# Rotary tables built with positions along the row, and a norm factor spread through DRAM, in a two-layer decoder trunk on one Trainium2 core

## The chip, the cores and the metric

The kernel runs on one core of one Trainium2 chip. The metric is the device time of one execution in microseconds, median of several runs; before the change it is 650.1 us (three runs, 649.99 to 650.54). The engines of the core are named as in the profile: PE (TensorE matmuls; PEld is its weight load), DVE (VectorE), ACT (ScalarE), POOL (GpSimd) and SP (SyncE, which only issues DMAs here).

## The reference

A trunk of two layers over 256 positions of width 1024, batch 1. Each layer is an attention mixer, a cross attention over 256 memory rows and a gated MLP with a short convolution, each behind an RMS norm and a residual. What the change touches:

```python
def rope(x, positions):
    half = HEAD_DIM // 2
    inv_freq = ROPE_THETA ** (-jnp.arange(half, dtype=jnp.float32) / half)
    ang = positions.astype(jnp.float32)[:, None, :, None] * inv_freq
    cos, sin = jnp.cos(ang), jnp.sin(ang)
    xf = x.astype(jnp.float32)
    x1, x2 = xf[..., :half], xf[..., half:]
    return jnp.concatenate([x1 * cos - x2 * sin, x2 * cos + x1 * sin], axis=-1).astype(x.dtype)
...
# layer 0: heads 0-7 stick-breaking (no rotary), heads 8-15 block-sparse with rotary q and k
o_moba = moba_attention(rope(q[:, N_SB_HEADS:], positions),
                        rope(k[:, N_SB_HEADS:], positions), v[:, N_SB_HEADS:])
...
# every layer: cross attention reads rmsnorm(mem)
h = h + memory_cross_attention(rmsnorm(h, norm_xa_g[layer]), rmsnorm(mem, norm_mem_g[layer]), ...)
```

A head is 64 wide, so there are 32 frequencies. The RMS norm's gains are folded into what is multiplied, and its factor, one number for each row (position or memory row), is applied to results.

## The kernel before

**Layout.** Activations lie turned: 128 features on the partitions, the 256 positions along the row (`P` = 128, `T` = 256). Two heads of 64 share a tile of 128 partitions. Every fp32 product is made of three matmuls (line 303): weights and activations are split into a rounded part (`whi`, `xh`) and a rest (`wlo`, `xl`). Weights come in blocks of 128x1024 by SP into `raw` (seven buffers); ACT writes `whi` in two halves (line 134), DVE `wlo` (line 135), five buffers each. So each block of weights costs PE 24 matmuls, ACT two copies and DVE two subtractions.

**Order.** PE's order is the program's order, written by hand: `VISITS` and a `Pipe` that counts half-steps of the projection loop say after which projection a pair of heads is multiplied, weighed and summed. DVE, ACT, POOL and SP are ordered by the framework's scheduler from the same program; each engine then runs its own queue strictly in that order.

**Layer 0's mixer** (up to about 110 us) projects q and k of eight pairs of heads and v of four groups. Pairs 0 to 3 are stick-breaking (`Stick`): PE multiplies q and k and adds a mask (lines 378 to 383), ACT and DVE make `s` (lines 388 to 391) and split it into `sp` (ACT line 393, DVE line 394), PE multiplies `sp` by a triangle (lines 399, 401), ACT takes the exponential `pt` (line 403), PE multiplies `pt` by v (line 450). Pairs 4 to 7 are softmax heads whose q and k are rotated first.

**Rotary tables.** `rope_angles` (line 465) puts the positions on the partitions, 128 by 2, and makes a 128x64 tile of angles (two times 32 frequencies). The angle is reduced to a turn around zero in many small steps on DVE: rounding by a large constant (lines 478, 479), splitting the count of turns in two (481, 482) and subtracting pieces of two pi (486); a clamp ends it (489). It is a generator; a step of it runs at each half-step of the pipe. `rope_sines` (line 495) loads ACT's table for the sine, takes four sines, of the angle and of half the angle for each half of the positions, each with the 32 frequencies repeated four times so that a tile of 128x128 results, and loads the table of exponentials and logarithms again. `rope_tables` (line 506) turns the four tiles by PE's transposes into 128 features by 256 positions, copies them out of PSUM on ACT (with a sign by feature for the sine; the half angle's sine is squared), and DVE makes cos = 1 - 2 sin^2(half) and both tables times the row's norm factor (`scaled`). For pair 4 the tables are used after the swap of halves (`rope`, POOL and DVE), for pairs 5 to 7 in the evacuation itself (`evac_turned`).

**The memory's factor.** `mem.rows` loads the memory's rows and squares them (half on ACT, half on DVE); `mem.sums` makes the factor as a column, 128x2 (`rcol`: DVE line 280, a power on POOL line 284). `mem.spread` (line 288) makes it a row on all partitions (`rrow`): two PE transposes of a broadcast column (line 291) into the `po` bank and an ACT copy (line 294). Its readers are the evacuations of the memory's keys, `mk` (line 354).

Of the kernel before, what the change touches and what calls it, by code (L numbers as in the profile page):

```python
# [9 lines left out]
F32 = mybir.dt.float32  # L10
F32R = mybir.dt.float32r
BF16 = mybir.dt.bfloat16
I32 = mybir.dt.int32
AF = mybir.ActivationFunctionType
ALU = mybir.AluOpType
AX = mybir.AxisListType

P = 128
T = 256
D = 1024  # L20
KD = D // P
DH = 64
# [21 lines left out]
C_CONV = 64  # L44
C_BF = C_CONV + 2 * 4 * 2 * KF
C_FREQ = C_BF + 1
C_SIGN = C_FREQ + DH // 2
N_SMALL = C_SIGN + 1


# [29 lines left out]
def trunk(ctx: ExitStack, tc: tile.TileContext, a: dict, out: bass.AP):  # L80
    nc = tc.nc
# [9 lines left out]
    act = pool("act", 1)  # L91
    parts = pool("parts", 1)
    qkv = pool("qkv", 1)
    xin = pool("xin", 1)
    shift(64)
    wsp = pool("wsp", 5)
    tmp = pool("tmp", 2)
# [5 lines left out]
    NX, NG, NP, NB = 8, 16, 12, 8  # L103

    def bank(pl, tag, width=512):
        return pl.tile([P, 512], F32, tag=tag, name=tag)[:, :width]
# [7 lines left out]
    def order(later, earlier):  # L114
        tc.add_manual_dep(later.ins, earlier.ins.name,
                          mybir.DependencyInfo(mybir.DependencyClass.NoSync, mybir.DependencyReason.DATA),
                          reason="order")
# [121 lines left out]
    class Stats:  # L239
# [45 lines left out]

        def spread(self, ps=None):
            ps = ps or self.ps
            for t in range(2):  # L290
                nc.tensor.transpose(ps[:, t * P:(t + 1) * P], self.col[:, t:t + 1].broadcast_to([P, P]), ident)
            bufs = 1 if self.keep else 2
            self.row = act.tile([P, T], F32, tag="rrow" + self.keep, name="rrow", bufs=bufs)
            nc.scalar.copy(self.row, ps[:, :T])
# [168 lines left out]
    cos = cst.tile([P, T], F32, name="cos")  # L463

    def rope_angles():
        f = lambda n, dt=F32: xin.tile([P, T], dt, tag="gh", name=n, bufs=NG)[:, :DH]
        pi, ang, kk, kh = f("ri", I32)[:, :2], f("ra"), f("rk"), f("rh")
        pf = kk[:, :2]
        nc.sync.dma_start(pi, a["positions"])
        eng = nc.vector  # L470
        yield
        eng.tensor_copy(pf, pi)
        for t in range(2):
            eng.tensor_scalar(ang[:, t * DH // 2:(t + 1) * DH // 2], small[:, C_FREQ:C_SIGN], pf[:, t:t + 1], None,
                              op0=ALU.mult)
        for parts in (True, False):
            yield
            eng.tensor_scalar(kk, ang, 1.0 / TWO_PI, MAGIC, op0=ALU.mult, op1=ALU.add)
            eng.tensor_scalar(kk, kk, -MAGIC, None, op0=ALU.add)
            if parts:  # L480
                eng.tensor_scalar(kh, kk, MAGIC * 2048.0, -MAGIC * 2048.0, op0=ALU.add, op1=ALU.add)
                eng.tensor_tensor(kk, kk, kh, op=ALU.subtract)
            for c in _pieces():
                yield
                for n in (kh, kk) if parts else (kk,):
                    eng.scalar_tensor_tensor(ang, n, -c, ang, op0=ALU.mult, op1=ALU.add)
        yield
        pi_f = float(np.nextafter(np.float32(np.pi), np.float32(0)))
        eng.tensor_scalar(ang, ang, pi_f, -pi_f, op0=ALU.min, op1=ALU.max)
        angles.append(ang)  # L490

    angles = []


    def rope_sines(prev):
        s = tmp.tile([P, 2, 2, 4, DH // 2], F32, tag="wide", name="rs", bufs=5)
        for i, scale in enumerate((1.0, 0.5)):
            for t in range(2):
                x = angles[0][:, t * DH // 2:(t + 1) * DH // 2]
                prev, last = nc.scalar.activation(s[:, i, t], x.unsqueeze(1).broadcast_to([P, 4, DH // 2]), AF.Sin,  # L500
                                                  scale=scale), prev
                order(prev, last)
        order(nc.scalar.preload_act_table_set("natural_log_exp_and_others"), prev)
        angles.append(s)

    def rope_tables(st):
        ps = bank(psA, "acc")
        for i in range(4):
            nc.tensor.transpose(ps[:, i * P:(i + 1) * P], angles[1][:, i // 2, i % 2].rearrange("p a f -> p (a f)"),
                                ident)  # L510
        nc.scalar.activation(sin, ps[:, :T], AF.Copy, scale=small[:, C_SIGN:C_SIGN + 1])
        nc.scalar.activation(cos, ps[:, T:], AF.Square)
        nc.vector.tensor_scalar(cos, cos, -2.0, 1.0, op0=ALU.mult, op1=ALU.add)
        both = tmp.tile([P, 2 * T], F32, tag="wide", name="scaled", bufs=5)
        for i, x in enumerate((cos, sin)):
            scaled.append(both[:, i * T:(i + 1) * T])
            nc.vector.tensor_mul(scaled[i], x, st.row)
# [91 lines left out]
    def mixer(layer, st, xs):  # L609
# [20 lines left out]
        def visit(out, prod, weigh):  # L630
            if out:
                res = heads_out([(heads[n], pairs[n][2], (n % 2) * P) for n in out])
                for n, pr in zip(out, res):
                    outs[n] = pr
            for n in prod:
                q, k, _ = pairs[n]
                heads[n] = [Stick(i, q, k) if layer == 0 and n < 4 else
                            Soft(i, q, k, decays[2 * n + i] if decays else None) for i in range(2)]
            both_products([hd for n in prod for hd in heads[n]])
            for n in weigh:  # L640
                for i, hd in enumerate(heads[n]):
                    hd.weigh(nc.vector.tensor_copy if n > 5 and i else nc.scalar.copy)
            if layer == 0 and pipe.now == 8:
                rope_tables(st)
            if layer == 0 and pipe.now == 17:
                mem.spread(bank(psO, "po"))
            for n in prod:
                for hd in heads[n]:
                    hd.scores()

        if layer == 0:
            pipe.at(13, mem.sums)
            pipe.at(6, lambda: rope_sines(heads[1][1].last))
        for step, *work in VISITS[layer]:
            pipe.at(step, lambda work=work: visit(*work))

        for g in range(4):
# [27 lines left out]
            if g == 0 and layer == 0:  # L685

                accs = [accS() for _ in range(4)]
                for n, (xh, xl) in enumerate(xs):
                    b, o = b0[n // 2], (n % 2) * 4 * P
                    steps = [(b.hi, xh), (b.hi, xl), (b.lo, xh)]  # L690
                    for group in ((0, 1), (2, 3)) if n < 2 else (range(4),):
                        for m, (wt, x) in enumerate(steps):
                            for i in group:
                                product(accs[i], wt[:, o + i * P:o + (i + 1) * P], x, n == 1 and m == 2 and i == 3,
                                        start=n == 0 and m == 0, stop=n == KD - 1 and m == 2)
                b = [block(w[i]) for i in (2, 3, 6)]
                nc.sync.dma_start(const[:, :T], a["const"][:, :T])
                st.rows(a["xt"])
                b.append(block(w[7]))
                st.sums()  # L700
                pv = [proj_nat(b, xs, t, accA()) for t in range(2)]
                early = proj(b[2], 0, xs, accA(), hooks={9: lambda: st.spread(bank(psO, "po"))})
                late_constants()
                v = [evac_col(ps, st, t, "v", 6) for t, ps in enumerate(pv)]
                for i in range(2):
                    q, k = (evac_row(accs[2 * i + j], st, "qk"[j], j == 0) for j in range(2))
                    launch(i, q, k, v)
                steps = rope_angles()
                next(steps)
                for i in range(12):  # L710
                    pipe.at(1 + i // 3, lambda: next(steps, None))
                continue
            elif g == 0:
                f = bank(psO, "po", T)

                def rates():
                    gates(f)
                    st.sums()

                q, more = pair(0, ({20: rates}, {15: st.spread}))  # L720
                k = more()
                q, k = evac_row(q, st, "q", True), evac_row(k, st, "k", False)
                decay = decay_rows(f, st)
            else:
                q, k = pair(0)
# [358 lines left out]
def _layout(inp):  # L1084
# [19 lines left out]
    d["x"] = c(kt(inp["x"][0].T).reshape(P, -1))  # L1104
    d["mem"] = c(kt(inp["mem"][0].T).reshape(P, -1))
    d["xt"], d["memt"] = (c(inp[n][0].reshape(2, P, D)) for n in ("x", "mem"))
    d["positions"] = c(inp["positions"][0].reshape(2, P).T)
    d["ab_in"] = qkv(inp["ab_w_in"][0])
    k = kt(inp["ab_w_in"][0]).transpose(1, 0, 2)
    d["ab_first"] = c(np.concatenate([k[:, :, j * P:(j + 1) * P] for j in (0, KD, 1, KD + 1)], axis=2))  # L1110
# [24 lines left out]
            small[:, C_CONV + l * 8 * KF + i:C_CONV + (l + 1) * 8 * KF:4] = vec(v)  # L1135
    small[:16, C_BF] = inp["fox_b_f"][0]
    freq = (10000.0 ** (-np.arange(DH // 2) / (DH // 2))).astype(np.float32)
    small[:, C_FREQ:C_SIGN] = freq
    small[:, C_SIGN] = np.where(np.arange(P) % DH < DH // 2, -1.0, 1.0)
    d["small"] = small  # L1140
    const = np.zeros((P, N_CONST), np.float32)
# [26 lines left out]
```

## Time and profile before

| | |
|---|---|
| median of three runs | 650.1 us |
| the profiled execution's own time | 651.21 us |
| its span, from the first to the last instruction | 649.4 us |
| mean granted TensorE clock | 0.998 |
| moved by DMA | 124.02 MB |

The span is what the profile's times count from. A row of the timeline has the start in us, the length of the group in us, engine, line, operation, result <- operands, and the count of instructions; square brackets hold the idle time ahead and what ended it. A row of a line or tile has the count and the shortest, median and longest duration in ns, then the first and last start. Neighbouring instructions of an engine overlap, so the spacing of starts and the duration of one are different numbers.

### The profile page before, as it was taken

To read this page: it belongs to the slowest core of one execution; us is meant where nothing else is said; L and a number is where in the kernel's file an instruction comes from. 1 tells how busy PE (TensorE), PEld (TensorE's weight loads), DVE (VectorE), ACT (ScalarE), POOL (GpSimd) and SP (SyncE) were. 2 spreads that over 40 slices of the span, in tenths; PEclk is the share of its full clock that TensorE was granted. 3 is DMA by queue.
4 is the path that set the end of the run, shared out by engine and by line. 5 is a ranking of instruction groups with operands and counts; after the bars stand their busy time and mean duration, and the time that the engine had idled before them with its cause. 6 is when DMAs were issued, how large, how long until landed. Compare 5 with 4: busy or idle time off the path is not lost.

```text
span 649.4 us, 14609 instructions
## 1 busy us (share of the span) xinstructions
PE 641.0 (99%) x5635; PEld 627.5 (97%) x5635; DVE 531.5 (82%) x1106; ACT 433.2 (67%) x871; POOL 71.2 (11%) x84
## 2 busy tenths in 40 slices
PE   8999999999999999999999999999999999999996
PEld 6999999999999999999999999999999999999996
DVE  5879995999999999856578977769999999896442
ACT  6789774777787777554464776557878776784332
POOL 0001000316100000011114210022350000000000
PEclk9999999999999999999999999999999999999999
DMA  8967661645566666666649654326365667696501
GB/s 309 393 229 245 200 206 34 198 161 194 162 197 202 219 206 187 183 192 206 204 158 313 209 170 153 132 77 192 110 242 182 192 207 206 174 338 197 194 1 66
DMA packets 47669, 124.02 MB, mean 191 GB/s; under 512 B 13648, under 2 KB 17520, under 8 KB 47600
## 3 DMA queue, kind: packets, MB, share of 16 engines
q1 hardware_dynamic: 47168, 122.53, 58.5%
q8 instruction: 44, 0.72, 0.4%
q10 hardware_dynamic: 432, 0.56, 0.2%
q14 instruction: 25, 0.20, 0.1%
HBM read 119.90 MB, written 1.07 MB: 186 GB/s over the span
## 4 chain that ended last, share of the span: by engine, by line
PE 96%; DMA 2%; issue 1%; ACT 0%; DVE 0%; POOLq 0%; POOL 0%; ACTq 0%; DVEq 0%
PE acc L303 49%; PE sc L303 28%; PE acc L1009 3%; PE sc L1009 3%; PE po L1009 2%; PE po L450 2%; PE po L303 2%; PE sc L415 1%; PE sc L435 1%; DMA h<-x 1%; DMA raw<-ab_first 1%; PE sc L798 1%; PE sc L821 1%; PE sc L399 0%; PE acc L301 0%
## 5 line engine op out<-in xcount | busy, mean ns | idle before, releaser
L135 DVE TENSOR_TENSOR wlo<-raw,whi 128x512 fp32r<-128x512 f32 (+2 forms) x288 | 268.2, 953 | 56.5 <-ACT whi L134 53.4
L134 ACT ACTIVATE whi<-raw 128x512 fp32r<-128x512 f32 (+2 forms) x288 | 225.4, 815 | 90.2 <-PE acc L303 37.1
L303 PE MATMUL sc<-xn,whi 128*128 128x256 f32 x656 | 112.9, 276 | 0.0
L303 PEld LDWEIGHTS sc<-xn,whi 128*128 128x128 f32 x656 | 98.7, 188 | 0.0
L303 PE MATMUL sc<-xn,wlo 128*128 128x256 f32 x328 | 90.5, 276 | 0.0
L303 PE MATMUL acc<-xh,whi 128*128 128x256 f32 x287 | 80.7, 281 | 0.0
L303 PE MATMUL acc<-xn,whi 128*128 128x256 f32 x464 | 80.3, 276 | 0.0
L303 PE MATMUL acc<-xl,whi 128*128 128x256 f32 x288 | 79.8, 277 | 0.0
L303 PE MATMUL acc<-xh,wlo 128*128 128x256 f32 x283 | 78.6, 278 | 0.0
L303 PEld LDWEIGHTS acc<-xn,whi 128*128 128x128 f32 x464 | 69.8, 188 | 0.0
L303 PE MATMUL acc<-gh,whi 128*128 128x256 f32 x240 | 67.0, 279 | 0.0
L303 PE MATMUL acc<-gl,whi 128*128 128x256 f32 x240 | 66.2, 277 | 0.0
L303 PE MATMUL acc<-gh,wlo 128*128 128x256 f32 x236 | 65.1, 276 | 0.0
L303 PE MATMUL acc<-xn,wlo 128*128 128x256 f32 x232 | 64.0, 276 | 0.0
L252 POOL TENSOR_TENSOR sq<-sq 128x256 f32<-128x256 f32 x35 | 30.1, 861 | 302.1 <-ACT sq L246 286.2
L303 PEld LDWEIGHTS sc<-xn,wlo 128*128 128x128 f32 x328 | 61.6, 188 | 0.0
L303 PEld LDWEIGHTS acc<-xh,whi 128*128 128x128 f32 x287 | 54.0, 188 | 0.4
L303 PEld LDWEIGHTS acc<-xl,whi 128*128 128x128 f32 x288 | 54.2, 188 | 0.0
L303 PEld LDWEIGHTS acc<-xh,wlo 128*128 128x128 f32 x283 | 53.2, 188 | 0.0
L303 PEld LDWEIGHTS acc<-gh,whi 128*128 128x128 f32 x240 | 45.1, 188 | 1.1 <-ACT gh L182 0.8
L303 PEld LDWEIGHTS acc<-gl,whi 128*128 128x128 f32 x240 | 44.9, 188 | 0.0
L303 PEld LDWEIGHTS acc<-gh,wlo 128*128 128x128 f32 x236 | 44.3, 188 | 0.0
(283 smaller groups left out, 1531.1 us busy)
## 6 DMA issues: line engine op xcount, KB each, us to landing
raw<-up SPq DMA_DIRECT2D x88, 512.0 KB, 4.2
raw<-fox_in SPq DMA_DIRECT2D x24, 512.0 KB, 4.1
raw<-down_rows SPq DMA_DIRECT2D x22, 512.0 KB, 4.3
raw<-ab_in SPq DMA_DIRECT2D x20, 512.0 KB, 7.2
raw<-down SPq DMA_DIRECT2D x16, 448.0 KB, 3.3
raw<-ab_out SPq DMA_DIRECT2D x8, 512.0 KB, 4.4
raw<-down SPq DMA_DIRECT2D x8, 512.0 KB, 3.6
raw<-fox_out SPq DMA_DIRECT2D x8, 512.0 KB, 4.3
```

What stands on the lines that cost most here:

```text
L134: i = nc.scalar.activation(hi[:, s], raw[:, s], AF.Copy)
L135: j = nc.vector.tensor_sub(lo[:, s], raw[:, s], hi[:, s].bitcast(F32))
L252: nc.gpsimd.tensor_tensor(sq, sq, self.acc, op=ALU.add)
L303: nc.tensor.matmul(ps, st, mv, **kw)
L415: nc.tensor.matmul(s[:, c], q[:, qs], k[:, 0:n], start=i == 0, stop=True, skip_group_check=True)
L435: nc.tensor.transpose(self.s[:, c:c + P], self.p[:, c:c + P], ident)
L450: nc.tensor.matmul(po[i * DH:(i + 1) * DH, j * T + q:(j + 1) * T], v[m][:, vc + i * DH:vc + (i + 1) * DH], hd.pt[:, c], start=m == 0 and j ...
L798: nc.tensor.matmul(s[:, t * T:(t + 1) * T], self.q[:, t * P:(t + 1) * P], self.k, start=t == 0, stop=True, skip_group_check=True)
L821: nc.tensor.transpose(self.s[:, m * T + t * P:m * T + (t + 1) * P], self.p[:, t * T + m * P:t * T + (m + 1) * P], ident)
L1009: nc.tensor.matmul(ps[:, o:o + T], x[:, s], y[:, c + o:c + o + T], start=False, stop=k == KF - 1 and x is gl, skip_group_check=True)
```

## The change

Two parts, both in layer 0's mixer.

The angles are made where they are needed: positions run along the row (a broadcast DMA brings all 256 to every partition), and the frequency is a column, one number for each partition. Angles are a 128x256 tile, every step of the reduction covers it, and the two sines come out in their final layout: the sine with its sign as the scale, the half angle's sine with scale 0.5, squared in place. Four ACT sines become two, PE's four transposes and one ACT copy go. The steps of `rope_angles` are spread over five half-steps of the pipe in place of four.

The memory's factor goes to DRAM and back: `leave` writes the column as 256 numbers, `come` reads them as a row broadcast to all partitions. Both are DMAs on SP; the two PE transposes and the ACT copy go. `sums` stays at step 13 of the pipe, `leave` is at 15, `come` at 17.

```diff
+        def leave(self):
+            self.kept = far.tile([2, P], F32, name="factors")
+            nc.sync.dma_start(self.kept.rearrange("t p -> p t"), self.col)
+
+        def come(self):
+            self.row = act.tile([P, T], F32, tag="rrow" + self.keep, name="rrow", bufs=1)
+            nc.sync.dma_start(self.row, self.kept.rearrange("t p -> (t p)").partition_broadcast(P))
...
     def rope_angles():
-        f = lambda n, dt=F32: xin.tile([P, T], dt, tag="gh", name=n, bufs=NG)[:, :DH]
-        pi, ang, kk, kh = f("ri", I32)[:, :2], f("ra"), f("rk"), f("rh")
-        pf = kk[:, :2]
-        nc.sync.dma_start(pi, a["positions"])
+        f = lambda n, dt=F32: xin.tile([P, T], dt, tag="gh", name=n, bufs=NG)
+        pi, ang, kk, kh = f("ri", I32), f("ra"), f("rk"), f("rh")
+        nc.sync.dma_start(pi, a["positions"].partition_broadcast(P))
         eng = nc.vector
         yield
-        eng.tensor_copy(pf, pi)
-        for t in range(2):
-            eng.tensor_scalar(ang[:, t * DH // 2:(t + 1) * DH // 2], small[:, C_FREQ:C_SIGN], pf[:, t:t + 1], None,
-                              op0=ALU.mult)
+        eng.tensor_copy(ang, pi)
+        eng.tensor_scalar(ang, ang, col(C_FREQ), None, op0=ALU.mult)
...
     def rope_sines(prev):
-        s = tmp.tile([P, 2, 2, 4, DH // 2], F32, tag="wide", name="rs", bufs=5)
-        for i, scale in enumerate((1.0, 0.5)):
-            for t in range(2):
-                x = angles[0][:, t * DH // 2:(t + 1) * DH // 2]
-                prev, last = nc.scalar.activation(s[:, i, t], x.unsqueeze(1).broadcast_to([P, 4, DH // 2]), AF.Sin,
-                                                  scale=scale), prev
-                order(prev, last)
+        for x, scale in ((sin, small[:, C_SIGN:C_SIGN + 1]), (cos, 0.5)):
+            prev, last = nc.scalar.activation(x, angles[0], AF.Sin, scale=scale), prev
+            order(prev, last)
         order(nc.scalar.preload_act_table_set("natural_log_exp_and_others"), prev)
-        angles.append(s)
 
     def rope_tables(st):
-        ps = bank(psA, "acc")
-        for i in range(4):
-            nc.tensor.transpose(ps[:, i * P:(i + 1) * P], angles[1][:, i // 2, i % 2].rearrange("p a f -> p (a f)"),
-                                ident)
-        nc.scalar.activation(sin, ps[:, :T], AF.Copy, scale=small[:, C_SIGN:C_SIGN + 1])
-        nc.scalar.activation(cos, ps[:, T:], AF.Square)
+        nc.scalar.activation(cos, cos, AF.Square)
...
-            if layer == 0 and pipe.now == 17:
-                mem.spread(bank(psO, "po"))
...
             pipe.at(13, mem.sums)
+            pipe.at(15, mem.leave)
+            pipe.at(17, mem.come)
...
-                    pipe.at(1 + i // 3, lambda: next(steps, None))
+                    pipe.at(1 + 5 * i // 12, lambda: next(steps, None))
```

On the host the positions stay a plain row and the table of small numbers holds one frequency for each partition (355 columns in its late part in place of 386).

The lines move by up to eight from the matmul helper on (303 is 311 in the changed kernel). PE, behind the masks of the second pair of stick-breaking heads, before:

```order
L383 MATMUL sc<-masks 128x128
L509 MATMUL acc<-const,rs 128x128 x4
L303 MATMUL acc<-xh,whi 128x256
L303 MATMUL acc<-xl,whi 128x256
L303 MATMUL acc<-xh,wlo 128x256
```

and in the changed kernel:

```order
L391 MATMUL sc<-masks 128x128
L311 MATMUL acc<-xh,whi 128x256
L311 MATMUL acc<-xl,whi 128x256
L311 MATMUL acc<-xh,wlo 128x256
L311 MATMUL acc<-xh,whi 128x256
```

The four transposes are gone and nothing stands in their place; the two of the factor (line 291) go in the same way, and PE's order is otherwise unchanged.

DVE, at the last two `s` and `sp` of the first two pairs of heads (tiles `s_528` and `s_537`), before:

```order
L266 ISA raw,ssq<-raw 128x512
L266 ISA ssq 128x1
L489 TENSOR_SCALAR ra<-ra 128x64
L266 ISA raw,ssq<-raw 128x512
L266 ISA ssq 128x1
L391 SCALAR_TENSOR_TENSOR s_528<-sc,s_528 128x384
L391 SCALAR_TENSOR_TENSOR s_537<-sc,s_537 128x384
L394 TENSOR_TENSOR sp<-s_528,sp 128x384
L135 TENSOR_TENSOR wlo<-raw,whi 128x512
L394 TENSOR_TENSOR sp<-s_537,sp 128x384
L352 SCALAR_TENSOR_TENSOR q<-acc,rrow 128x256
L354 TENSOR_TENSOR k<-acc,rrow 128x256
```

and in the changed kernel (there `s_527` and `s_536`):

```order
L266 ISA raw,ssq<-raw 128x512
L266 ISA ssq 128x1
L402 TENSOR_TENSOR sp<-s_527,sp 128x384
L399 SCALAR_TENSOR_TENSOR s_536<-sc,s_536 128x384
L491 SCALAR_TENSOR_TENSOR ra<-rk,ra 128x256
L360 SCALAR_TENSOR_TENSOR q<-acc,rrow 128x256
L491 SCALAR_TENSOR_TENSOR ra<-rk,ra 128x256
L402 TENSOR_TENSOR sp<-s_536,sp 128x384
L491 SCALAR_TENSOR_TENSOR ra<-rk,ra 128x256
L135 TENSOR_TENSOR wlo<-raw,whi 128x512
L494 TENSOR_SCALAR ra<-ra 128x256
L362 TENSOR_TENSOR k<-acc,rrow 128x256
```

The last steps of the angles (`ra`, 128x256 now) have moved down among and behind these `sp`, and one squared half of the memory (`ISA`, line 266, with the read of its sum behind it) has moved behind the last one; the evacuation of q (line 360 there) has moved ahead of it.

ACT, around the two loads of its tables, before:

```order
L393 ACTIVATE sp<-s_537 128x384
L500 ACT_TABLE_LOAD
L500 ACTIVATE rs<-ra 128x128 x4
L503 ACT_TABLE_LOAD
L134 ACTIVATE whi<-raw 128x512
L403 ACTIVATE pt<-sc 128x384
L268 ACTIVATE raw,ssq<-raw 128x512
L403 ACTIVATE pt<-sc 128x384
L134 ACTIVATE whi<-raw 128x512
L403 ACTIVATE pt<-sc 128x384
L134 ACTIVATE whi<-raw 128x512
L403 ACTIVATE pt<-sc 128x384
```

and in the changed kernel:

```order
L134 ACTIVATE whi<-raw 128x512
L401 ACTIVATE sp<-s_536 128x384
L134 ACTIVATE whi<-raw 128x512 x3
L502 ACT_TABLE_LOAD
L502 ACTIVATE sin<-ra,small 128x256
L502 ACTIVATE cos<-ra 128x256
L504 ACT_TABLE_LOAD
L411 ACTIVATE pt<-sc 128x384 x4
L507 ACTIVATE cos<-cos 128x256
L134 ACTIVATE whi<-raw 128x512 x6
```

Five `whi` copies that stood behind the loads are now ahead of them, as is the squaring of the memory's other half, and the four `pt` follow the second load one after another.

On SP, the write of the factor stands between two weight blocks ahead of pair 4's first swap, and its read behind pair 4's swaps, ahead of the memory's key weights.

More of the change, by code (lines that the diff above doesn't have):

```diff
@@ L46 @@
 C_FREQ = C_BF + 1
-C_SIGN = C_FREQ + DH // 2
+C_SIGN = C_FREQ + 1
 N_SMALL = C_SIGN + 1
@@ L1106, in _layout @@
     d["xt"], d["memt"] = (c(inp[n][0].reshape(2, P, D)) for n in ("x", "mem"))
-    d["positions"] = c(inp["positions"][0].reshape(2, P).T)
+    d["positions"] = c(inp["positions"][0])
     d["ab_in"] = qkv(inp["ab_w_in"][0])
@@ L1137, in _layout @@
     freq = (10000.0 ** (-np.arange(DH // 2) / (DH // 2))).astype(np.float32)
-    small[:, C_FREQ:C_SIGN] = freq
+    small[:, C_FREQ] = np.tile(freq, P // (DH // 2))
     small[:, C_SIGN] = np.where(np.arange(P) % DH < DH // 2, -1.0, 1.0)
```

## The prediction

> **What bounds the kernel now.** I read the page's busy shares first, then the slices, then the chain of work that ended last.
>
> ```profile
> span 649.4 us, 14609 instructions
> PE 641.0 (99%) x5635; PEld 627.5 (97%) x5635; DVE 531.5 (82%) x1106; ACT 433.2 (67%) x871; POOL 71.2 (11%) x84
> ...
> PE   8999999999999999999999999999999999999996
> ...
> DVE  5879995999999999856578977769999999896442
> ...
> PE 96%; DMA 2%; issue 1%; ACT 0%; DVE 0%; POOLq 0%; POOL 0%; ACTq 0%; DVEq 0%
> ```
>
> TensorE is busy 99% of the span and carries 96% of the final chain, so the kernel is a stream of matmuls that hardly ever waits. Only two things can change the time: fewer or shorter matmuls, or a new wait of TensorE. The second is the danger, because in the slices of the first mixer VectorE shows 9 as well. The two stretches that the change touches, by the table of windows (busy us of PE, PEld, DVE, ACT, POOL, then the granted clock, DMA share and GB/s):
>
> ```profile
> 25.00:45.00 20.00, 20.00 (x179) 19.66 (x179) 17.83 (x55) 16.99 (x38) 0.00 (x0) 1.00 0.87 317
> 45.00:55.00 10.00, 10.00 (x100) 9.21 (x99) 7.50 (x15) 9.99 (x23) 0.70 (x1) 1.00 0.64 210
> ```
>
> PE has no idle time in either, at full clock. DVE has 2.2 us free of 20 in the first stretch, where the angles are made, and ACT none in the second, where the two table loads lie.
>
> **What is removed from TensorE.** Six transposes go: four of the sines, two of the memory's factor. What they cost is read from starts, not from durations. The first two rows are the same place one pair of heads earlier, without transposes.
>
> ```profile
> 30.59 0.55 PE L383 MATMUL sc<-masks 128*128 128x128 bf16 x7
> 30.95 0.36 PE L303 MATMUL acc<-whi,xh 128*128 128x256 f32 x1
> ...
> 53.09 0.55 PE L383 MATMUL sc<-masks 128*128 128x128 bf16 x7
> 53.48 0.61 PE L509 MATMUL acc<-const,rs 128*128 128x128 f32 x4
> 53.85 0.36 PE L303 MATMUL acc<-xh,whi 128*128 128x256 f32 x1
> ...
> 84.81 0.60 PE L435 MATMUL sc<-const,s 128*128 128x128 f32 x4
> 85.25 0.38 PE L291 MATMUL po<-const,rcol 128*128 128x128 f32 x2
> 85.39 0.36 PE L303 MATMUL acc<-whi,xh 128*128 128x256 f32 x1
> ```
>
> From the masks to the next product take 30.95 - 30.59 = 0.36 us without the four transposes and 53.85 - 53.09 = 0.76 with them: 0.40 us. The two of the factor follow other transposes of the same kind: four starts in 85.25 - 84.81 = 0.44, so 0.11 each, 0.22 for two. Together **0.62 us**, all on the path, since PE waits for nothing around them. The PSUM bank that the sines took and the `po` bank of the spread become free too; nobody waits for them in these rows, so I give that nothing.
>
> A transpose's own duration is 0.27 us (four in 0.61 with starts 0.11 apart, so the last takes 0.61 - 0.33). [...] It is a rival below, worked out from the rows alone.
>
> **What is added to VectorE.** The angles become 128x256 instead of 128x64. Rows of today's shape, and rows of the same operations at 128x256:
>
> ```profile
> L486 DVE SCALAR_TENSOR_TENSOR ra<-rk,ra x8: 214/218/226, 30.1 to 38.2; 128x64 f32<-128x64 f32 x8
> L478 DVE TENSOR_SCALAR rk<-ra x2: 184/190/195, 27.4 to 34.3; 128x64 f32<-128x64 f32 x2
> ...
> L513 DVE TENSOR_SCALAR cos<-cos x1: 290/290/290, 57.6 to 57.6; 128x256 f32<-128x256 f32 x1
> L517 DVE TENSOR_TENSOR scaled<-cos,rrow x1: 426/426/426, 57.9 to 57.9; 128x256 f32<-128x256 f32 x1
> ...
> 24.88 0.29 DVE L173 CAST signs<-const 128x256 fp32r<-128x256 f32 x1
> 25.08 0.22 DVE L175 CAST masks<-const 128x128 bf16<-128x128 f32 x1
> 25.22 0.16 DVE L472 CAST rk<-ri 128x2 f32<-128x2 int32 x1
> 25.42 0.39 DVE L474 TENSOR_SCALAR ra<-small,rk 128x32 f32<-128x32 f32 x2
> 25.72 0.42 DVE L352 SCALAR_TENSOR_TENSOR q<-sc,rrow 128x256 f32<-128x256 f32 x1
> 26.05 0.41 DVE L354 TENSOR_TENSOR k<-sc,rrow 128x256 f32<-128x256 f32 x1
> ```
>
> A row's successor starts about 0.09 before its end (25.72 + 0.42 = 26.14, next start 26.05), so an operation takes its duration less 0.09. Twelve three-operand steps grow from 0.13 to 0.33: 2.4 us. Six scalar steps grow from 0.10 to 0.20: 0.6. One subtraction of two tensors, 0.2. The cast grows by about 0.1 and the two small products become one, 0.1 less. No row shows a cast of int32 at this width; it lies between 0.16 (the small one) and about 0.42 (an operation at full width), and I take 0.29, the cast row of that width. The sum is **3.2 us** more on DVE between 25 and 45 us, against 2.2 free. So I follow the order of the changed kernel up to the work that PE wants soonest: the last `sp` of the second pair of heads.
>
> ```profile
> 40.72 0.56 DVE L391 SCALAR_TENSOR_TENSOR s<-sc,s 128x384 f32<-128x384 f32 x1 [0.48 <-ACT s L390]
> 41.20 0.55 DVE L394 TENSOR_TENSOR sp<-s,sp 128x384 fp32r<-128x384 f32 x1
> 41.66 0.69 DVE L135 TENSOR_TENSOR wlo<-raw,whi 128x512 fp32r<-128x512 f32 x1
> 42.26 0.55 DVE L394 TENSOR_TENSOR sp<-s,sp 128x384 fp32r<-128x384 f32 x1
> ...
> 43.88 0.57 PE L399 MATMUL sc<-sp,signs 128*128 128x384 f32 x2
> ```
>
> Today that `sp` ends at 42.81, and PE's second product at 43.88 (0.23 behind the first, so 44.11) is its first reader: 1.3 us of slack. In the new order, from the cast's start at 25.22 to the start of that `sp`, DVE has: cast 0.33 with its successor waiting for it, one scalar product 0.20, seven evacuations of q and k at 0.33 (2.31), five scalar steps at 0.20 (1.0), the subtraction 0.33, eleven of the twelve three-operand steps at 0.33 (3.63), eleven `wlo` at 0.60 (41.66 to 42.26; 6.6), four `s` at 0.47 and three `sp` at 0.46 (3.26), and one squared half of the memory, 0.61. That is 18.3 us, so it starts at 43.5 and ends at 44.05, 0.06 before its reader. The other squared half, one three-operand step and the clamp stand behind it in the new order, the idle 0.48 is filled, and one evacuation of q comes ahead; on balance that pays for more than half of the growth. I count **no wait** here, with 0.4 either way for eighteen microseconds added up from rows: up to 0.3 us of wait.
>
> **What is moved on ScalarE.** The sines wait for the angles, and the four exponentials that PE multiplies next (`pt`) now stand behind both table loads with no other work between.
>
> ```profile
> 42.05 1.28 ACT L500 ACT_TABLE_LOAD   x1
> 43.34 0.91 ACT L500 ACTIVATE rs<-ra 128x128 f32<-128x128 f32 x4
> 44.26 1.28 ACT L503 ACT_TABLE_LOAD   x1
> 45.55 0.63 ACT L134 ACTIVATE whi<-raw 128x512 fp32r<-128x512 f32 x1
> 46.09 0.47 ACT L403 ACTIVATE pt<-sc 128x384 f32<-128x384 f32 x1
> ...
> 48.86 0.50 ACT L403 ACTIVATE pt<-sc 128x384 f32<-128x384 f32 x1
> ...
> 50.06 1.08 PE L450 MATMUL po<-pt,v 128*64 128x256 f32 x8
> ```
>
> Today the last `pt` ends at 49.36 and PE starts on them at 50.06. In the new order the last copy of `sp` can start once its `s` is made, at 42.7 by the sum above; three `whi` follow (0.53 each, 45.55 to 46.09), so the first load starts at about 44.8 and ends at 46.1. The angles are ready by then: behind `sp` come 0.46 + 0.33 + 0.60 and a 0.29, 45.2. Two sines of 128x256 I take at 0.5 each (no row has them; four of half the size take 0.91, between 0.8 and 1.0 in all), the second load ends at 48.4, four `pt` at 0.4 end at 50.1. The fourth is not the first that PE reads, so this too just fits; it has 0.3 to 0.6 us left. ACT loses two 128x256 copies behind that and is never later again.
>
> **What is moved on the queues.** Positions become 128 KB instead of 1, the small table 16 KB less: 0.3 us at 400 GB/s.
>
> ```profile
> DMA to landing us min/median/max: 7.0/7.0/7.0
> ...
> SPq L130 <- DVE wlo L135: 29.5, 12, 7.4
> L354 DVE TENSOR_TENSOR mk<-acc,rrow x4: 411/418/425, 91.2 to 416.6; 128x256 f32<-128x256 f32 x4
> ```
>
> The positions, issued at 16.5, land at 23.5 (the first row is theirs), then 23.8, and the cast starts at 25.22. The weights behind them on SP wait for free buffers (second row: 29.5 us in the first 110), not the reverse. The write of the factor waits for POOL's power, at about 50, where SP issues a block of weights today; that block is used over 20 us later, and the rotated queries behind it wait for DVE and start where they do now. The read back goes out at about 58 and lands within some 8 us; its first reader is `mk` at 91.2. I cost all this at nothing; if the read came after 91 PE would wait for the rest.
>
> **Sum.** -0.62 + 0 on the profiled run's 651.21 (span 649.4, 1.8 around it) is 650.6; that run stood 1.1 over the median of 650.1, and the same step on the median gives **649.5 us**, -0.1%.
>
> **The rivals.**
> VectorE becomes the bound. If none of the growth is paid for by the moved work, `sp` ends at 42.81 + 3.2 = 46.0, PE waits 1.9 at 44.1, and the net is +1.3: **651.4**. It is slower than before from a wait of 0.62, that is from an `sp` that ends after 44.73. For it: DVE has less room than it is given. Against it: the new order carries three operations past the `sp`, and DVE today idles 0.48 there. A small wait, 0.3 to 0.6, would leave 650.0. Chance 0.14, half of it over 650.7.
> The full duration of the transposes is saved: 6 x 0.27 = 1.6 us, **648.5**. For it speaks only that nothing else fills PE; against it the starts 0.11 apart. [...] Chance 0.04.
> The gain is made up for later: a wait that PE alone doesn't set, such as the one between 125 and 130 us, ends when it did. Then **650.1**. Against it: DVE and ACT, which answer there, follow PE's products. Chance 0.08.
>
> **How the numbers follow.** My forecast has 0.74, its own range is 649.2 to 649.9. A measurement of this kernel can tell about 0.2% (1.3 us) from no change: faster means under 648.8, slower over 651.4. The faster side has only the full durations, 0.04; the slower one the upper end of the late `sp`, 0.05; the rest, 0.91, is no change. The range goes from 648.9 to 651.0, for the late `sp` and for the spread of the three runs (649.99 to 650.54).
>
> **What would show it.** PE's rows: the product behind the masks near 53 starts 0.03 behind the last mask, and the one near 85 follows the last transpose of the heads directly; neither has a wait. DVE: the last `sp` of the second pair ends between 43.7 and 44.5. ACT: the first load starts near 44.8, `pt` ends near 50.1. PE's row at 43.9 or 50.1 with a gap over 0.6 would make the prediction wrong, and so would a cast of the positions that waits for its DMA.

## The result, and the profile after

The changed kernel takes **656.5 us** (median of four runs, 655.7 to 657.5) against 650.3 (four runs, 649.99 to 650.54): ratio 1.0096, 95% interval 1.0083 to 1.0108. It is slower by 6 us, where 649.5 was forecast and 651.0 was the upper end of the range. The profiled execution took 657.08.

From the page of the changed kernel, the span, the busy shares, two rows of the slices and the shares of the chain that ended last:

```profile
span 655.3 us, 14593 instructions
...
PE 642.9 (98%) x5629; PEld 629.0 (96%) x5629; DVE 533.3 (81%) x1105; ACT 432.7 (66%) x867; POOL 71.7 (11%) x84
...
PE   8999799999999999999999999999999999999996
...
DVE  6898497899999999866668988859999999996442
...
PE 84%; DMA 7%; DVE 4%; ACT 2%; issue 1%; SPq 0%; POOL 0%; POOLq 0%; ACTq 0%; DVEq 0%
```

The shares of busy time hardly moved. The fifth slice of PE (66 to 82 us) is what shows: 7 in place of 9, with DVE at 4 in place of 9, and the chain now passes through DMA and DVE. The table of windows of the changed kernel, in the columns of the prediction (busy us of PE, PEld, DVE, ACT, POOL, then granted clock, DMA share, GB/s):

```profile
50.00:55.00 5.00, 5.00 (x55) 4.36 (x52) 4.97 (x11) 5.00 (x13) 0.00 (x0) 1.00 0.56 22
55.00:60.00 5.00, 5.00 (x45) 5.00 (x44) 4.87 (x12) 4.79 (x12) 0.00 (x0) 1.00 0.32 28
...
70.00:75.00 5.00, 3.92 (x38) 3.26 (x37) 0.00 (x0) 3.01 (x8) 0.00 (x0) 1.00 0.90 322
75.00:80.00 5.00, 1.84 (x13) 1.47 (x15) 4.27 (x9) 1.61 (x5) 0.00 (x0) 0.92 0.50 159
80.00:85.00 5.00, 5.00 (x36) 4.78 (x34) 5.00 (x12) 0.00 (x0) 0.00 (x0) 0.74 0.84 246
```

and the first two of them before:

```profile
50.00:55.00 5.00, 5.00 (x56) 4.27 (x55) 5.00 (x10) 5.00 (x12) 0.00 (x0) 1.00 0.89 295
55.00:60.00 5.00, 5.00 (x47) 5.00 (x46) 4.84 (x13) 4.58 (x12) 1.21 (x2) 1.00 0.34 76
```

Read them from left to right in time. From 50 to 60 us PE is full in both, but DMA has nearly stopped: 22 and 28 GB/s in place of 295 and 76. Twenty microseconds later DVE does nothing for five (0.00 in 70 to 75), then PE is idle, then it runs at a lower granted clock. So the cause lies near 50 and the loss near 75. The list of DMA issues from 49 to 56 us, each with KB and the median us from issue to landing, says what stopped; the changed kernel:

```profile
raw<-ab_in SPq DMA_DIRECT2D x2, 512.0 KB, 12.4
turned<-q SPq DMA_DIRECT2D x4, 32.0 KB, 11.0
turned<-k SPq DMA_DIRECT2D x1, 32.0 KB, 11.7
factors<-rcol SPq DMA_DIRECT2D x1, 1.0 KB, 9.0
```

and before:

```profile
raw<-ab_in SPq DMA_DIRECT2D x2, 512.0 KB, 4.2
turned<-q SPq DMA_DIRECT2D x4, 32.0 KB, 3.5
turned<-k SPq DMA_DIRECT2D x3, 32.0 KB, 2.2
```

The write of one kilobyte takes 9.0 us, and everything issued behind it up to 56 us takes 11 to 12 in place of 2 to 4, the swaps too (`turned`, which go from SBUF to SBUF and touch no DRAM). How that reaches PE, by SP's queue (timeline and waits, changed kernel), DVE's timeline and PE's:

```profile
49.45 0.38 SPq L290 DMA_DIRECT2D factors<-rcol  x1
49.92 0.43 SPq L130 DMA_DIRECT2D raw<-ab_in  x1
51.03 2.50 SPq L518 DMA_DIRECT2D turned<-q  x4
53.62 0.53 SPq L130 DMA_DIRECT2D raw<-ab_in  x1
54.25 9.50 SPq L518 DMA_DIRECT2D turned<-k  x4
...
66.97 1.16 SPq L518 DMA_DIRECT2D turned<-q  x2
```

```profile
SPq L518 <- DMA factors<-rcol: 3.7, 1, 3.7
SPq L518 <- DMA raw<-ab_in: 3.6, 1, 3.6
```

```profile
75.05 0.42 DVE L529 TENSOR_TENSOR q<-q,turned 128x256 f32<-128x256 f32 x1 [8.03 <-DMA turned<-q]
```

```profile
75.96 0.70 PE L423 MATMUL sc<-k,q 64*128 64x256 f32 x4 [2.04 <-DVE k L534]
78.86 1.81 PE L423 MATMUL sc<-k,q 64*128 64x256 f32 x12 [2.21 <-DVE k L529]
80.60 0.58 PE L311 MATMUL acc<-xh,whi 128*128 128x256 f32 x1
...
82.26 0.41 PE L311 MATMUL acc<-xl,whi 128*128 128x256 f32 x1
82.47 0.34 PE L311 MATMUL acc<-xh,wlo 128*128 128x256 f32 x1
82.65 0.28 PE L311 MATMUL acc<-xh,whi 128*128 128x256 f32 x1
```

Before, SP issued the four swaps of pair 4's k in a row:

```profile
54.78 2.43 SPq L523 DMA_DIRECT2D turned<-k  x4
...
60.60 1.78 SPq L523 DMA_DIRECT2D turned<-q  x3
```

Now the second of them waits 3.7 us until the factors have landed, and the third 3.6 more until the block behind them has; so pair 5's q is swapped at 66.97 instead of 60.60. Why SP stops there can be counted in its rows: the second swap is the eighth DMA behind the write (a block, four swaps of q, a block, two swaps of k), the third is the eighth behind that block, and the waits for `raw<-xa_k` that SP has later, at pair 5's k, have the same distance. In the changed kernel's trace none of SP's 324 DMAs goes out before the one eight places before it has landed: the second swap goes out at 58.48, the factors have landed at 58.47, and the third at 62.60, when the block has landed at 62.59. The trace of before shows the same for its 322; in both they carry eight semaphore numbers. DVE keeps the order of its queue here: it stands 8.03 us at pair 5's sum, with pair 4's last step (`k`, line 534) behind it, and PE waits 2.04 us for that step. The 2.21 us that follow are a wait for pair 5's k (line 529): PE multiplies the two pairs in one stretch, and pair 5's k is swapped from 70.65 on, where before it was from 63.78. Nothing is wrong with the memory's factor itself: its row lands at 70.6, and `mk` reads it at 99.1.

### The profile page after: what moved, and what is told of

Same layout as the page of the kernel before. It is cut to its first block, busy times and chain, and to the rows that moved or that the text cites. A ratio compares the mean times of both kernels' runs of the same rounds, so it can differ in the third digit from the quotient of the medians.

```text
span 655.3 us, 14593 instructions
## 1 busy us (share of the span) xinstructions
PE 642.9 (98%) x5629; PEld 629.0 (96%) x5629; DVE 533.3 (81%) x1105; ACT 432.7 (66%) x867; POOL 71.7 (11%) x84
## 4 chain that ended last, share of the span: by engine, by line
PE 84%; DMA 7%; DVE 4%; ACT 2%; issue 1%; SPq 0%; POOL 0%; POOLq 0%; ACTq 0%; DVEq 0%
PE acc L311 41%; PE sc L311 27%; PE acc L1004 3%; PE sc L1004 3%; PE po L1004 2%; DMA turned<-q 2%; PE po L311 2%; PE po L458 1%; DVE wlo L135 1%; DMA raw<-xt 1%; DMA raw<-xa_k 1%; PE sc L423 1%; PE sc L443 1%; DMA h<-x 1%; ACT whi L134 1%
```

## The experiments

Three theories were set against each other. **W**: the write, 256 numbers of 4 bytes each, keeps the DMA engines busy for 9 us. **Q**: SP's queue is late because the write waits there for POOL's power. **A**: the wider angles make DVE late. Within W there are two more. **N**: pieces that are neighbours in DRAM are written one after the other. **C**: each small piece has a price, wherever it goes.

**1. The angles alone.** The trip through DRAM is taken out, and PE spreads the factor as before.

```diff
+            if layer == 0 and pipe.now == 17:
+                mem.spread(bank(psO, "po"))
...
-            pipe.at(15, mem.leave)
-            pipe.at(17, mem.come)
```

> The new angles alone; the memory's factor is spread by PE's transposes as before. Theory W (the write of the factor as 256 numbers of 4 bytes holds the DMA engines, 9.0 us to landing in the changed kernel): 650.0, between 649.4 and 650.6, PE without a wait near 74 us. Theory Q (SP's queue stands still while it waits for POOL's factor): the same 650. Theory A (the wider angles are late on DVE and everything behind them): about 656.

650.75 us (10 runs, 650.5 to 651.9) against 650.43; ratio 1.0004, interval 0.9995 to 1.0014. PE has no wait near 75, so A falls as the cause of the 6 us. It does take something: PE's only wait that this half of the change makes is the second product of the last `sp`,

```profile
43.79 0.44 PE L399 MATMUL sc<-sp,signs 128*128 128x384 f32 x1 [0.29 <-DVE sp L394]
```

and that eats most of the 0.40 that the four transposes save.

**2. The trip alone**, in the kernel before, with its own angles: `leave` at step 15 and `come` at step 17 as in the change's diff, `spread` out.

> The trip of the factor through DRAM alone; angles and turned sines as before. Theory W and theory Q: about 656 (655 to 658), the write lands 9 us after its issue, PE waits some 4 us near 74. Theory A: 650, as before.

653.4 us (9 runs, 651.4 to 656.0), ratio 1.0045, interval 1.0030 to 1.0061. The write lands after 10.4 us, the swaps of q behind it after 6.6 at the median:

```profile
turned<-q SPq DMA_DIRECT2D x4, 32.0 KB, 6.6
turned<-k SPq DMA_DIRECT2D x1, 32.0 KB, 6.5
factors<-rcol SPq DMA_DIRECT2D x1, 1.0 KB, 10.4
```

So the trip loses time without the angles too. It is half as much, with a write that goes out 1.8 us earlier (47.6). Among pair 4's swaps of k SP stops once there, 2.9 us for the factors; the block behind them has landed when the third swap is due. PE waits 0.6 us for a k at 74.7 and 1.7 us in four waits for DVE's softmax (`s`) between 84 and 88, and the granted clock stays at 1.00. What sets the difference between the two starts of the write was not varied.

**3. One packet in the same place.** The changed kernel, in which only one partition's two numbers are written, 8 bytes in one piece, at the same place of SP's queue and behind the same wait; PE spreads the factor.

```diff
-            self.kept = far.tile([2, P], F32, name="factors")
-            nc.sync.dma_start(self.kept.rearrange("t p -> p t"), self.col)
+            self.kept = far.tile([1, 2], F32, name="factors")
+            nc.sync.dma_start(self.kept, self.col[0:1])
```

> The changed kernel, but the write at the same place of SP's queue, behind the same wait for POOL, is 8 bytes from one partition (one packet in place of 256) and nothing reads it; the factor's row is made by PE's transposes. SP's order up to pair 4's swaps is that of the changed kernel. Theory W: the wait costs nothing, 650.0 (649.4 to 650.6), and the weight block behind the write lands about 4 us after its issue. Theory Q: 655 to 657. Theory A: 656.

650.59 us (10 runs), ratio 1.0003, interval 0.9994 to 1.0012. SP waits for POOL as long as in the changed kernel (3.2 us there), and nothing is lost:

```profile
SPq L290 <- POOL rcol L284: 3.1, 1, 3.1
```

Q falls. It is the writing of the numbers, not the waiting for them.

**4. Pairs.** All 256 numbers, but laid out as they stand in SBUF: one piece of 8 bytes for each partition, 128 pieces; the row is read back interleaved, and `mk` reads it with a stride.

```diff
-            self.kept = far.tile([2, P], F32, name="factors")
-            nc.sync.dma_start(self.kept.rearrange("t p -> p t"), self.col)
+            self.kept = far.tile([P, 2], F32, name="factors")
+            nc.sync.dma_start(self.kept, self.col)
```

> The changed kernel with the factor written as 128 pairs of 8 bytes that lie next to each other, and read back in that order (mk's evacuation reads the row with a stride). Theory W with a cost for each written piece: half the pieces, landing after 4 to 5 us, 651 to 654. Theory W with a cost by bytes or by place alone: as the changed kernel, 9 us, 656. Theory Q: 656. Theory A: 656.

650.27 us (10 runs), ratio 0.9999, interval 0.9989 to 1.0008: this one edit takes the whole loss away, with the change's two parts in place. The write lands in 3.4 us.

**5. Half the numbers.** Only one of the two columns is written, 128 pieces of 4 bytes, still neighbours; PE spreads the factor.

> As e3_one_packet, but what is written at that place is one column of the factor: 128 numbers of 4 bytes that lie next to each other (512 bytes). The factor's row is made by PE's transposes; nothing reads what is written. If each written piece costs the same, the landing is half the extra time of the changed kernel's 9.0 us, so 5 to 7 us; if 128 pieces are free whatever their size (as the 128 pairs were, 3.4 us), it is 3 to 4; if 4-byte pieces into one neighbourhood are slow whatever their count, about 9.

655.9 us (one run; 13 of the kernel before have a median of 650.5). The write lands in 8.2 us, so half the pieces take nine tenths of the time, and C, a price for each piece, falls.

**6 and 7. The 256 numbers apart**, 512 and 64 bytes from one to the next, PE spreading the factor; for 64:

```diff
+            self.kept = far.tile([2, P, 16], F32, name="factors")
+            nc.sync.dma_start(self.kept.rearrange("t p s -> p t s")[:, :, 0:1], self.col.unsqueeze(2))
```

> As e3_one_packet, but all 256 numbers of 4 bytes are written, each 512 bytes from the next. Theory N (the writes are slow because neighbours share a line of DRAM and wait for each other): landing 3 to 4.5 us and no wait of PE near 74. Theory C (a price for each small piece): 8 to 10 us as in the changed kernel, and PE waits or nearly.

> As f2_apart512 with 64 bytes between neighbours. Theory N with a line of 64 bytes or less: 3 to 4.5 us; with a larger line: between that and 9. Theory C: 8 to 10 us.

Both land in 1.6 us: 650.05 and 651.18 us (one run each; single runs of the kernel before lie between 649.9 and 651.5, so these two can't be told from it). The same number of pieces of the same size through the same queue cost next to nothing where no two lie less than 64 bytes apart.

**8. The write on POOL's queue**, in the changed kernel: `nc.gpsimd.dma_start` in place of `nc.sync.dma_start`, the numbers neighbours as in the change.

> The changed kernel with the same 256 numbers written from POOL's queue in place of SP's, so that SP waits neither for POOL nor for the write's landing. If the write holds the DMA engines themselves, the weight blocks and swaps behind it on SP still land late: 653 to 656. If only the queue that it stands in is held: 650 (649.4 to 650.8), with swaps landing within 5 us of their issue.

650.4 us (10 runs), ratio 0.9997, interval 0.9987 to 1.0006: no loss, although the write is as slow as before and the swaps that SP issues meanwhile are slow with it:

```profile
turned<-q SPq DMA_DIRECT2D x4, 32.0 KB, 6.5
turned<-k SPq DMA_DIRECT2D x4, 32.0 KB, 4.5
factors<-rcol POOLq DMA_DIRECT2D x1, 1.0 KB, 8.1
```

So SP's transfers land late behind the write also when it comes from another queue (6.5 us for a swap of q in place of 3.5). But SP, which begins pair 4's swaps at 50.81 here and at 51.03 in the changed kernel, has no 3.7 us wait for the factors in this run: it has sent all eight by 56, and pair 5's follow at 60.11 in place of 66.97. So W alone does not lose the 6 us.

```profile
53.55 2.41 SPq L518 DMA_DIRECT2D turned<-k  x4
...
60.11 1.95 SPq L518 DMA_DIRECT2D turned<-q  x2
```

This edit moves more than the write. SP no longer waits for POOL either, and two blocks of weights go out ahead of the write (46.8 and 48.4), where the changed kernel sends them behind it (49.92 and 53.62). That the write's hold becomes a delay of PE through SP, stopped until it has landed, is read from the changed kernel's rows; no run takes that stop away and leaves the blocks where they are.

**9 to 11. Between 4 and 64 bytes**: 8, 16 and 32 bytes from one number to the next.

> The write's 256 numbers of 4 bytes each, 8 bytes apart in DRAM (8 to a 64-byte line, 16 in the changed kernel), row side made by the removed PE spread. If pieces that share a 64-byte line are written one after the other (16 to a line took 9.0 us, one to a line 1.6), 8 to a line take about 4.5 to 5.5 us from issue to landing, and the span shows at most a short wait near 74 to 85 us, time 650 to 652. If what counts is that pieces touch without a gap, 1.6 us and 650. If the number of pieces in some larger neighbourhood decides, 8 to 10 us and the loss of the changed kernel, 655 to 657.

> The same 256 numbers 16 bytes apart, 4 to a 64-byte line. One after the other within a 64-byte line: about 2.5 to 3.5 us to land, 650. Within a 32-byte line (2 to a line): about 2 us. Touching pieces alone: 1.6 us. All three give no loss of time, about 650.

> The same 256 numbers 32 bytes apart, 2 to a 64-byte line. Within a 64-byte line: about 2 to 2.2 us to land; within a 32-byte line or by touching alone: 1.6 us as with 64 bytes. Time about 650 in each case.

They took 650.1, 651.1 and 651.4 us, one run each, which can't be told from before. These are the times from issue to landing of all layouts, one landing each:

| layout in DRAM | pieces x bytes | within 64 bytes | us to land |
|---|---|---|---|
| neighbours (the change) | 256 x 4 | 16 | 9.0 |
| neighbours, one column | 128 x 4 | 16 | 8.2 |
| pairs, neighbours | 128 x 8 | 8 | 3.4 |
| 8 bytes apart | 256 x 4 | 8 | 3.4 |
| 16 bytes apart | 256 x 4 | 4 | 2.3 |
| 32 bytes apart | 256 x 4 | 2 | 2.0 |
| 64 and 512 bytes apart | 256 x 4 | 1 | 1.6 |

The more pieces share 64 bytes, the longer it takes; the total hardly counts (9.0 and 8.2, and 3.4 twice). That it is 64 bytes and not 32 rests on 0.4 us between two single landings (2.0 and 1.6). That carries N, but not as it was put: a fixed price for each further piece in 64 bytes would have given 4.5 to 5.5 at 8 bytes, and 3.4 was measured. From one piece to eight each adds about 0.26 us ((3.4 - 1.6) / 7), from eight to sixteen 0.7 ((9.0 - 3.4) / 8). Touching alone does not explain the step, since the pairs touch as well and land in 3.4. Whether it comes from sixteen pieces in 64 bytes or from two in 8 was not tried, nor what in the memory path does it.

**12. Pairs on POOL's queue**, the two cures together.

> The factor stored as 128 pairs of 8 bytes (one per partition) and read back by the broadcast, as in the run with pairs, with the write issued on POOL's queue, so that SP's queue does not wait for POOL's power. If the write's holding of the DMA engines is all that the change loses, this is at the best what the change's removed work is worth: 0.22 for two transposes beside a fold and at most 0.40 for four beside the first angles, of which 0.3 to 0.4 is spent by the second product's wait for DVE: about 650.0, not to be told from before, ratio 0.998 to 1.000. If the queue behind the wait still cost something in the run with pairs on SP's queue (650.3), it is 0.2 to 0.4 lower here than that.

650.45 us (11 runs) against 650.33, ratio 1.0002, interval 0.9993 to 1.0011. The write lands in 4.8 us there. Taking SP out of the wait brings nothing more, and no version measured beats the kernel before by more than the noise.

## Why the prediction was wrong

**The step that failed** is the one on the queues: "The write of the factor waits for POOL's power, at about 50, where SP issues a block of weights today; that block is used over 20 us later, and the rotated queries behind it wait for DVE and start where they do now. ... I cost all this at nothing". The wait was costed rightly, as the run with one packet shows, and so was the block's slack. What the step left out is the write's own duration, 9.0 us. It priced when SP issues, never how long 256 pieces take to land or that what is issued behind them lands late with them (11 to 12 us), and it took one kilobyte for nothing. Nor did it count that SP stops here with eight DMAs under way (3.7 and 3.6 us). So the overlap that it counted on, swaps that "start where they do now", was not there: pair 4's first swaps are issued in the changed kernel at 51.03, even earlier than before, and land at 62.8 to 63.3; the fourth swap of its k goes out at 63.2. The prediction gave the read back "some 8 us" as a guess (5.0 was measured) and the write none, although a write of many small pieces was an operation that no row of before shows, and had to be bounded from both sides. None of the rivals was this one, so the range had no room for it. The positions were no part of it: they land 7.1 us after their issue, 7.0 before, and the 400 GB/s that they were costed at is near the 393 that the page of before shows in its second slice.

**The size**, from the starts of the same products in the two profiles, after less before. Ahead of the change's stretch, from 13.6 us on, the difference is -0.71; 0.4 of it is a wait of PE at 13.56 that only this profile of before has. Just ahead of the scores it is -0.29 (72.40 in place of 72.69). The product behind the scores of pairs 4 and 5 starts at 80.60 in place of 75.65:

```profile
75.65 0.39 PE L303 MATMUL acc<-xh,whi 128*128 128x256 f32 x1
...
76.79 0.28 PE L303 MATMUL acc<-xh,whi 128*128 128x256 f32 x1
```

That is +4.95, so 5.2 us are lost in the two waits (4.25) and in scores at a lower clock. At the second row it is 82.65 in place of 76.79, +5.86, so another 0.9 from products 0.21 apart in place of 0.11. Between the second wait and there the granted clock is one half for 3.4 us,

```profile
79.19:82.59 3.40, 3.40 (x21) 3.15 (x18) 3.40 (x8) 0.00 (x0) 0.00 (x0) 0.50 0.75 247
```

which is worth 1.7 us, an estimate: half of 3.4. Waits and clock make 5.95 of the 6.15 us between -0.29 and +5.86. Before the factor's transposes (85 us before, 91.5 after) it has grown to +6.54, 0.2 of it in a further wait; the transposes that are gone then give 0.17 back, and it ends at +5.9, the difference of the spans.

**TensorE's terms were right.** Four transposes fewer: from -0.29 to -0.69 (53.16 in place of 53.85) over the masks near 53, 0.40 as forecast. Two fewer: 0.17, forecast 0.22. The starts, not the durations, gave the price. In place of the transposes nothing stands:

```profile
52.73 0.62 PE L391 MATMUL sc<-masks 128*128 128x128 bf16 x8
53.16 0.36 PE L311 MATMUL acc<-xh,whi 128*128 128x256 f32 x1
```

**VectorE's sum was right, its slack a little short.** From the cast of the positions to the start of the last `sp` of the second pair pass 18.4 us, forecast 18.3. It was to end at 44.05; it does at 43.66, since the cast starts 0.6 us earlier. But PE is earlier still: the first product below was at 43.88 before.

```profile
24.66 0.29 DVE L479 CAST ra<-ri 128x256 f32<-128x256 int32 x1
...
43.10 0.56 DVE L402 TENSOR_TENSOR sp<-s,sp 128x384 fp32r<-128x384 f32 x1
```

```profile
43.15 0.39 PE L407 MATMUL sc<-sp,signs 128*128 128x384 f32 x1
43.72 0.44 PE L407 MATMUL sc<-sp,signs 128*128 128x384 f32 x1 [0.17 <-DVE sp L402]
```

The second product starts 0.57 behind the first where 0.23 is usual, so PE loses 0.34 there; the prediction counted no wait, with up to 0.3. The rival with a net of +1.3 did not come, only its small form, a wait of 0.3 to 0.6. This small wait takes back more than half of what the six transposes give (0.57), and the rest, some 0.2 us, is less than the runs can show: the timed ones without the loss lie at 650.3 to 650.8.

**ScalarE's plan was right.** The two table loads start at 44.52 and 46.65 (forecast: near 44.8 and at 47.1), the two sines take 0.51 and 0.40 (0.5 each), and the four `pt` end at 49.6 (50.1); PE does not wait for them:

```profile
44.52 1.28 ACT L502 ACT_TABLE_LOAD   x1
...
46.65 1.28 ACT L504 ACT_TABLE_LOAD   x1
47.95 1.64 ACT L411 ACTIVATE pt<-sc 128x384 f32<-128x384 f32 x4
```

## What to carry to other kernels

In these runs a DMA had two prices, when its queue issues it and how long it and what is issued behind it take to land; bytes told neither. Ask of each new one how many pieces it is cut into and how close to one another they land: here a kilobyte as 256 neighbouring 4-byte writes took 9.0 us to land, with the swaps and blocks behind it landing after 11 to 12 us in place of 2 to 4, and as 8-byte pairs 3.4. Look also at which queue can't go on until such a transfer has landed: on POOL's queue the same slow write (8.1 us) cost nothing, and in the changed kernel's trace it is SP's stop behind it that reaches TensorE.

## What was not expected of the hardware

In these runs small writes were slow by how near they lie, not by their number: 128 neighbours of 4 bytes take 8.2 us, 256 that are 64 bytes apart 1.6. Their size alone is not the price either: the same 256 pieces of 4 bytes take 9.0 us as neighbours, and at 64 bytes apart, where eight of them share 512 bytes, they land as fast as those 512 apart (1.6 both).

Behind a write that is slow by its layout in DRAM (9.0 us, where 1.6 is enough for the same pieces 64 bytes apart), transfers that touch no DRAM were late too: the swaps from SBUF to SBUF took 11.0 us at the median behind it and a block of weights, in place of 3.5. In the run with the write on POOL's queue, where no block goes out between the two, they land from 57.8 us on, right behind the write (57.6).

Two waits of PE of 2.04 and 2.21 us, with four products between them, were followed by a granted clock of 0.50 from 79.19 to 82.59 and of 1.00 from 82.60 on. In the run with half the numbers it is 1.00 up to 85 us and 0.88 in the mean from 85 to 90, with four waits of PE for DVE's softmax, 1.7 us in all, the longest 0.64, and that is part of this single run's 655.9. In the run with the trip alone four waits of the same length (1.7 us in all, the longest 0.64) stand at 84 to 88 us, and the clock is 1.00 in every measured stretch up to 90; so the waits alone do not decide it. What does was not shown.
